# A decoder step on one core: sampled-attention copies, exponentials, convolution stores, turns and loads rearranged

## The chip, the core and the metric

The program runs on one NeuronCore of a Trainium2 chip. That core has five engines with an instruction stream each: TensorE (PE, the matrix products; its weight loads are shown apart as PEld), VectorE (DVE), ScalarE (ACT), GpSimd (POOL) and SyncE (SP), which here only issues transfers. An engine works through its stream in order and stops at an instruction whose operands aren't ready. Transfers between HBM and the on-chip memory SBUF run on DMA engines of their own; the products land in PSUM, of which the program keeps a few banks in rotation. The metric is the device time of one execution in microseconds, as the median of several runs.

## The reference

One inference step of a one-layer decoder, for 2048 new tokens of a prompt and for 8 sampled sequences with 8 new tokens each and 8192 cached ones. Everything is float32.

```python
z = x @ w_in                                   # one projection, 3600 columns
fq, fk, fv, flogf = ...                        # 8 attention heads of 64, with a forget gate
conv = conv_b + sum(xpad[:, j:j + S] * conv_w[j] for j in range(4))
mq, mk = split(silu(conv))                     # 4 mLSTM heads of 128
fox_h = softmax(q k^T / 8 + forget, causal) v  # prompt: 2048 keys; sampled: 8192 paged keys + 8 new ones
m_h   = mlstm(mq, mk, mv, ig, lf)              # chunked, with states C, n, m
mix = concat(fox_h, norm(m_h) * og) @ w_o
x1  = layer_norm(ALPHA * x + mix)
y   = layer_norm(ALPHA * x1 + square(relu(x1 @ w1)) @ w2)
```

Outputs are `y` for both token sets, the new keys, values and forget values, the mLSTM states and the convolution's last inputs.

## The kernel before

A float32 product is made of three products of rounded parts: every operand is split into a rounded high part (ACT, `split_hi`, line 149) and the rest (DVE, `split_lo`, line 152), and `mm3` (lines 157 to 159) multiplies high by high, low by high and high by low. So each piece of weights that comes in costs one ACT and one DVE pass before TensorE can use it.

The work has four stages, one after the other.

**Projection** (`block_a`, about 0 to 905 us), in four blocks of 512 tokens; the first block takes the 64 sampled tokens along. Each block does a first set of value columns, the columns that go through the convolution (`streamed`, in pairs of 128 columns with `ready` and `out`), then output gates, attention queries, keys and values. `pieces` goes over the weights in slabs of two or four 128-row chunks and for each slab over the token tiles; a `hook` may do something ahead of a tile's product. Before a block can begin, its tokens must be loaded (`x_load`), turned by TensorE (`x_turn`, line 370, into PSUM tile `px`) and split. The tiles `px` and `pm` share four PSUM banks; a bank comes free once ACT has copied the product in it (`stage`, line 587). The prompt's mLSTM (`m_block`) and the sampled one (`m_sample`) are generators of which a step is taken every 2.3 us of estimated product time (`PACE_M`, in `tick`); the sampled attention (`sample_attention`) is another generator, with a step every 5.6 us (`PACE_A`) here and every 5 (`PACE_C`) later.

**Prompt attention** (`phase_b`, about 905 to 1325 us): for a head and a group of 256 queries, `scores`, `weights` and `values`, a unit behind one another. `keys` doubles a head's keys (`dup`: a transfer, and a GpSimd copy for the second half, in `twice`), turns and splits them.

**Output projection** (`phase_o`, to about 1550 us) and the **MLP** (`phase_c`, `last_block`) follow. In the last tiles of the output projection the tokens of the first MLP block are turned (`x1_turn`, line 1403). The sampled attention goes on in these two stages.

`sample_attention` takes 32 steps a sequence. `k_gather` fetches 128 rows of keys by an indirect transfer from GpSimd, `k_turn` transposes them in place on DVE (line 2002), `qk_step` multiplies them (`sQ`, line 2025). At step 35 of a sequence `softmax` finds the maximum and takes ten exponentials one after the other (lines 2062 and 2064). `weights` (line 2094 on) then turns a quarter of them into PSUM tile `sT`, of which there is one, four transposes at a time, and copies the four into `PTs`: the copies of even number on DVE, the odd ones on ACT (line 2096). `pv_step` (`sO`, line 2137) multiplies `PTs` by values that were gathered by GpSimd (`v_gather`, line 2113).

The final order on each engine is made by a scheduler with a model of the time, from the data dependencies, the order in the code and `issue_after`, which holds an instruction behind another one. So a line's place in the code isn't its place in the stream.

Of the kernel before, what the change touches and what calls it, by code (L numbers as in the profile page):

```python
# [52 lines left out]
def body(ctx, tc, I, O, stages):  # L53
# [300 lines left out]
    def x_turn(bi, t):  # L354
# [12 lines left out]
        for hf in range(2):  # L367
            px = ppa.tile([128, 4, 128], F32, name="px", tag="pm", bufs=4)
            for k in range(4):
                T.transpose(px[:, k, :n], xn[:n, (hf * 4 + k) * 128:(hf * 4 + k + 1) * 128], ident[:n, :n])  # L370
# [145 lines left out]
    def block_a(bi):  # L516
# [26 lines left out]
        def pieces(sink, *cols, hook=None):  # L543
# [78 lines left out]
        J = {}  # L622

# [9 lines left out]
        def out(j, w, ps):  # L633
# [25 lines left out]
            if pre:  # L659
                ths = pa.tile([128, 64], F32, name="ths", bufs=1)  # L660
                conv(lambda q: J["qs"][:, :, q:q + 8], J["acs"], ths, ths)
                SY.dma_start(dqk[j], ths)
                V.tensor_copy(scT[:, j], J["qs"][:, :, 8:11])
# [4 lines left out]
        if pre:  # L668

# [82 lines left out]
    def b_first():  # L752
# [4 lines left out]
        G.tensor_copy(kn[:, :, 1], kn[:, :, 0])  # L757
# [6 lines left out]
        for g in range(4):  # L764
            for d in range(2):
                SY.dma_start(Bz["qn"][g][d * 64:d * 64 + 64], dq[0, 0:64, g * 256:(g + 1) * 256])
            if g == 1:
                SY.dma_start(kn[:, :, 0], O["k_prompt"].rearrange("l b s h d -> (l b s) (h d)")[512:1024, 0:64].rearrange("(i t) c -> t i c", t=128))
                G.tensor_copy(kn[:, :, 1], kn[:, :, 0])
# [64 lines left out]
    def m_block(bi):  # L834
# [7 lines left out]
        for _ in range(4):  # L842
# [229 lines left out]
    def phase_b():  # L1072
# [28 lines left out]
        def twice(src, t):  # L1101

            n = pb.tile([128, t, 2, 64], F32, name="dup", tag=f"dup{t}", bufs=3)
            SY.dma_start(n[:, :, 0], src.rearrange("(i t) c -> t i c", t=128))
            G.tensor_copy(n[:, :, 1], n[:, :, 0])
            return n

# [6 lines left out]

        def keys_load(h, g):
            return twice(kp[g * 512:(g + 1) * 512, h * 64:h * 64 + 64], 4)

        def keys(z, g):
# [3 lines left out]
            if not first:  # L1122
                kn = Bz["kn1"] if h == 0 and g == 1 else keys_load(h, g)
# [171 lines left out]
        for n in range(len(units) + 1):  # L1295
# [560 lines left out]
def sample_attention(tc, I, O, ps_, pps, cst, ident, sqk, dnl, dR, dmix, dqb, vx, kx, pe, ring_a):  # L1856
# [180 lines left out]
    def softmax(b):  # L2037
# [21 lines left out]
        for u in range(4):  # L2059
            for hg in range(2):  # L2060
                x = z["U"][u][:, hg].rearrange("p b k t -> p (b k t)")
                A.activation(x, x, AF.Exp, bias=m4[:, hg:hg + 1], accum_out=rp[:, hg, u:u + 1])
        for hg in range(2):
            A.activation(z["Sn"][:, hg], z["Sn"][:, hg], AF.Exp, bias=m4[:, hg:hg + 1], accum_out=rp[:, hg, 4:5])

    def softmax_new(b):

        z = state[b]
        rs = z["rs"] = ps_.tile([128, 2], F32, name="rs", bufs=2)
        V.tensor_reduce(rs, z["rp"], axis=AX.X, op=OP.add)  # L2070
# [15 lines left out]
    def weights(b, u, hg):  # L2086
# [8 lines left out]
        for f in range(4):  # L2095
            (A.copy if f % 2 else V.tensor_copy)(PT[:, hg, f].rearrange("p g h q -> p h g q"),
                                                 p[:, f].rearrange("p (h g q) -> p h g q", g=4, q=8))
# [72 lines left out]
    def step(n):  # L2170
# [30 lines left out]
        if b is not None and b < 8:  # L2201
            softmax_sum(b)
        u = at(n, 37, 8)
# [62 lines left out]
```

## Time and profile before

| | |
|---|---|
| median of three runs | 3270.63 us (3259.38 to 3270.8) |
| the profiled execution | 3264.98 us, of which the span from first to last instruction is 3263.1 |
| TensorE busy | 3174.9 us, 97% of the span |
| VectorE, ScalarE, GpSimd busy | 2230.5, 1393.6, 1049.9 us |
| mean granted TensorE clock | 0.990 |

The span is 88 us longer than TensorE is busy. The timeline of TensorE gives each of its waits with the engine that ended it; the table by windows shows the clock that was granted in a stretch, 1.00 being the full one.

### The profile page before, as it was taken

The page shows a single profiled execution, that of the slowest core. Times are in us where ns is not written, and L with a number is a line of the kernel's source. Part 1 is how long each engine was busy: PE and PEld are TensorE (multiplying, and loading weights), DVE is VectorE, ACT ScalarE, POOL GpSimd, SP SyncE. Part 2 cuts the span into 40 slices and gives each one's busy share as a digit, 9 for nine tenths or more (in the row PEclk, how much of TensorE's full clock was granted, in tenths as well). Part 3 has the DMA queues.
Part 4 walks back from the last instruction along what each step waited for, and adds up shares of the span by engine and source line. Part 5 has one row for each costly group of instructions (what it writes and reads, how often), then busy time and mean ns, then how long its engine had stood idle before and what let it go on. Part 6 is the DMA issues. An engine that isn't in the chain of part 4 may idle for free.

```text
span 3263.1 us, 54920 instructions
## 1 busy us (share of the span) xinstructions
PE 3174.9 (97%) x20140; PEld 2555.0 (78%) x20140; DVE 2230.5 (68%) x5239; ACT 1393.6 (43%) x2753; POOL 1049.9 (32%) x1171
## 2 busy tenths in 40 slices
PE   9999999999999999999999999999999999999998
PEld 8878787786777777777777777777777777799997
DVE  5857667666577777766566767666667545777777
ACT  4444244444377777412333333242423333454443
POOL 0011121432344444354333324323234210264441
PEclk9999999999999999999999999999999999999999
DMA  6565774977743224777686768776678645442221
GB/s 193 150 198 167 231 230 144 315 259 218 222 128 85 79 84 118 254 282 263 250 289 213 288 238 288 263 249 244 239 240 305 210 160 176 134 139 84 91 90 56
DMA packets 413845, 641.88 MB, mean 197 GB/s; under 512 B 83020, under 2 KB 295312, under 8 KB 412680
## 3 DMA queue, kind: packets, MB, share of 16 engines
q1 hardware_dynamic: 337320, 360.99, 36.4%
q0 software_dynamic: 74304, 270.57, 22.3%
q10 hardware_dynamic: 1952, 6.82, 0.6%
q8 instruction: 159, 2.61, 0.3%
q14 instruction: 110, 0.90, 0.1%
HBM read 585.43 MB, written 52.83 MB: 196 GB/s over the span
## 4 chain that ended last, share of the span: by engine, by line
PE 60%; DMA 5%; DVE 3%; issue 2%; POOL 1%; ACT 1%; SPq 0%; DVEq 0%; POOLq 0%; ACTq 0%
PE ph L157 7%; PE ph L158 7%; PE ph L159 7%; PE py L157 6%; PE py L159 6%; PE py L158 6%; PE po L1245 4%; PE pt L1228 4%; PE sO L2137 3%; PE pS L1187 2%; PE sQ L2025 2%; PE pS L1188 2%; DMA kT<-cache_k,idxK 2%; DMA xr<-cache_v,idxV 1%; PE pw L158 1%
## 5 line engine op out<-in xcount | busy, mean ns | idle before, releaser
L149 ACT ACTIVATE wh<-wr 128x1024 fp32r<-128x1024 f32 x268 | 277.6, 1056 | 538.2 <-PE py L159 299.8
L1996 POOL DMA_INDIRECT kT<-cache_k,idxK x256 | 262.3, 1025 | 741.1 <-PE sQ L2025 644.1
L2002 DVE STREAM_TRANSPOSE kT<-kT 128x512 f32<-128x512 f32 x512 | 330.2, 686 | 230.2 <-DMA kT<-cache_k,idxK 229.5
L157 PE MATMUL ph<-x1h,wh 128*128 128x512 f32 (+2 forms) x1280 | 453.5, 354 | 3.1 <-ACT xr L1664 2.1
L159 PE MATMUL ph<-x1h,wl 128*128 128x512 f32 (+2 forms) x1280 | 450.7, 354 | 6.0 <-DVE wl L152 6.0
L158 PE MATMUL ph<-x1l,wh 128*128 128x512 f32 (+2 forms) x1280 | 452.9, 354 | 0.0
L152 DVE TENSOR_TENSOR wl<-wr,wh 128x1024 fp32r<-128x1024 f32 x252 | 318.7, 1272 | 77.9 <-PE ph L159 45.8
L157 PE MATMUL py<-wh,h 128*128 128x512 f32 (+1 forms) x888 | 347.7, 395 | 0.8 <-DVE y L1807 0.3
L159 PE MATMUL py<-wh,h 128*128 128x512 f32 (+1 forms) x888 | 347.7, 392 | 0.0
L158 PE MATMUL py<-wl,h 128*128 128x512 f32 (+1 forms) x888 | 347.5, 392 | 0.0
L1607 DVE TENSOR_TENSOR y<-y,py 128x512 f32<-128x512 f32 x336 | 224.2, 677 | 142.6 <-PE py L159 140.6
L159 PEld LDWEIGHTS ph<-x1h,wl 128*128 128x128 f32 x1280 | 242.0, 189 | 38.9 <-DVE wl L152 7.1
L157 PEld LDWEIGHTS ph<-x1h,wh 128*128 128x128 f32 x1280 | 242.3, 189 | 38.1 <-ACT xr L1664 2.3
L158 PEld LDWEIGHTS ph<-x1l,wh 128*128 128x128 f32 x1280 | 242.1, 189 | 35.1 <-issue 2.5
L2113 POOL DMA_INDIRECT vt<-cache_v,idxV x156 | 160.6, 1030 | 291.0 <-PE sO L2137 252.1
L157 PE MATMUL pm<-whi,xhT 128*128 128x512 f32 (+2 forms) x648 | 235.7, 365 | 3.7 <-ACT acb L637 1.5
L158 PE MATMUL pm<-wlo,xhT 128*128 128x512 f32 (+2 forms) x648 | 230.7, 356 | 1.9 <-DVE wlo L152 1.9
L159 PE MATMUL pm<-whi,xlT 128*128 128x512 f32 (+2 forms) x648 | 230.6, 356 | 0.0
L157 PEld LDWEIGHTS py<-wh,h 128*128 128x128 f32 x888 | 167.1, 188 | 42.9 <-issue 7.8
L159 PEld LDWEIGHTS py<-wh,h 128*128 128x128 f32 x888 | 167.1, 188 | 36.2 <-issue 2.5
L158 PEld LDWEIGHTS py<-wl,h 128*128 128x128 f32 x888 | 167.1, 188 | 33.8 <-issue 2.9
L149 ACT ACTIVATE whi<-wra 128x1024 fp32r<-128x1024 f32 (+1 forms) x112 | 119.0, 1062 | 160.7 <-PE pm L159 105.6
(485 smaller groups left out, 7068.4 us busy)
## 6 DMA issues: line engine op xcount, KB each, us to landing
wr<-w SPq DMA_DIRECT2D x256, 512.0 KB
wra<-w_in SPq DMA_DIRECT2D x112, 512.0 KB
Rb<-dR SPq DMA_DIRECT2D x128, 128.0 KB
wr<-w_o SPq DMA_DIRECT2D x16, 512.0 KB
xr<-dmix SPq DMA_DIRECT2D x16, 512.0 KB
y<-x_prompt SPq DMA_DIRECT2D x16, 512.0 KB
dx<-y SPq DMA_DIRECT2D x16, 512.0 KB
qn<-dq SPq DMA_DIRECT2D x120, 64.0 KB
```

The costliest lines, as they stand in the source:

```text
L149: last["ACT"] = A.activation(dst, src, AF.Copy, scale=scale)
L152: r = (eng or V).tensor_tensor(dst, src, hi.bitcast(F32), op=OP.subtract)
L157: T.matmul(ps, wh, xh, start=first, stop=False, skip_group_check=free)
L158: T.matmul(ps, wh, xl, start=False, stop=False, skip_group_check=free)
L159: last["PE"] = T.matmul(ps, wl, xh, start=False, stop=stop, skip_group_check=free)
L1228: T.transpose(pt[:, k], sc[i][0][k0 // 8][:, (k0 % 8 + k) * 128:(k0 % 8 + k + 1) * 128], ident)
L1245: last["PE"] = T.matmul(po[c:c + 64, q0:], z["vn"][:, k], PTs[k // 4][:, k % 4, q0:], start=k == same[0], stop=k == same[-1], skip_group_c ...
L1607: V.tensor_tensor(y, y, ps, op=OP.add)
L1996: G.indirect_dma_start(out=piece(n), out_offset=None, in_=ck, in_offset=IO(ap=idxK[:, b, j // 2, j % 2:j % 2 + 1], axis=0))
L2002: V.transpose(x, x)
L2113: vx["last"] = G.indirect_dma_start(out=vt.rearrange("p f c -> p (f c)"), out_offset=None, in_=cv, in_offset=IO(ap=idxV[:, b, (kt % 4) * 4 ...
L2137: after_ = T.matmul(po[r:r + 32], z["PT"][:, hg, 2 * f + g, pg].rearrange("p h q -> p (h q)"), vts[f][:, g, hg * 256:(hg + 1) * 256], star ...
```

## The change

Line numbers here are those of the kernel before. Six edits, in the order of the code:

- **Turns.** `x_turn` returns its last transpose. For blocks 1 to 3 the first tile is turned ahead of the last tile's product of the last slab, and that product is held behind these transposes; the second tile is turned behind the last product.
- **Sampled convolution.** The eight results `ths` lie in one tile of eight slots and are stored by one transfer, not by eight from one reused tile.
- **First loads of prompt attention.** `b_first` is cut in two: the loads (`b_load`) are asked for at the first slab of the last value columns, the GpSimd copies and casts at the third slab's second tile.
- **`m_block`** waits six steps, not four, between asking for `gsb` and taking its exponential.
- **Keys.** The load (`keys_load`) and the GpSimd copy are parted; the load is asked for a unit earlier.
- **Sampled attention.** One ACT copy moves all four turned pieces into `PTs`. The exponentials are taken in four portions over steps 36 to 39, and the row sum is taken at step 40.

```diff
@@ x_turn
-                T.transpose(px[:, k, :n], xn[...], ident[:n, :n])
+                r = T.transpose(px[:, k, :n], xn[...], ident[:n, :n])
...
+        return r
@@ pieces
-                    if hook:
-                        hook(rows[0][0], i)
+                    r = hook(rows[0][0], i) if hook else None
                     if rows[0][0] == 0:
                         banks[t] = bank(t, n)
-                    part(banks[t], t, rows)
+                    with ExitStack() as es:
+                        if r is not None:
+                            es.enter_context(tc.issue_after(r.ins))
+                        part(banks[t], t, rows)
@@ convolution
+        if pre:
+            J["ths"] = ps_.tile([128, 8, 64], F32, name="ths", tag="vt", bufs=2)
...
-                ths = pa.tile([128, 64], F32, name="ths", bufs=1)
+                ths = J["ths"][:, j]
                 conv(lambda q: J["qs"][:, :, q:q + 8], J["acs"], ths, ths)
-                SY.dma_start(dqk[j], ths)
...
         if pre:
+            SY.dma_start(dqk.rearrange("j p t -> p j t"), J["ths"])
@@ turn_first
             if bi == 3:
-                if k == 4 and n == 0:
+                if k == 0 and n == 0:
+                    b_load()
+                if k == 4 and n == 1:
                     b_first()
                 return
...
-            if k == 6 and n == len(blk) - 2:
-                x_turn(bi + 1, BLKS[bi + 1][0])
+            if k == 6 and n == len(blk) - 1:
+                r = x_turn(bi + 1, BLKS[bi + 1][0])
                 x_load(BLKS[bi + 1][3])
-            if k == 6 and n == len(blk) - 1:
+                return r
+        pieces(halves(sink), (1024, 512), hook=turn_first)
+        if bi < 3:
+            with tc.issue_after(last["PE"].ins):
                 x_turn(bi + 1, BLKS[bi + 1][1])
-        pieces(halves(sink), (1024, 512), hook=turn_first)
@@ m_block
         va, Wm, qa = m_load(bi * 4)
-        for _ in range(4):
+        for _ in range(6):
             yield 1
         A.activation(gsb, gsb, AF.Exp)
@@ phase_b
+                if h == 0 and g in (1, 3):
+                    keys_load(0, g // 2 + 2)
+                if h < 7 and 3 <= g < 7:
+                    keys_load(h + 1, g - 3)
@@ weights of the sampled attention
-        for f in range(4):
-            (A.copy if f % 2 else V.tensor_copy)(PT[:, hg, f].rearrange("p g h q -> p h g q"),
-                                                 p[:, f].rearrange("p (h g q) -> p h g q", g=4, q=8))
+        A.copy(PT[:, hg].rearrange("p f g h q -> p f h g q"), p.rearrange("p f (h g q) -> p f h g q", g=4, q=8))
@@ step
+        b, u = divmod(n - 36, 32)
+        if 0 <= b < 8 and u < 4:
+            exps(b, u)
...
+        b = at(n, 40, 32)
+        if b is not None and b < 8:
+            z = state[b]
+            z["rs"] = ps_.tile([128, 2], F32, name="rs", bufs=2)
+            V.tensor_reduce(z["rs"], z["rp"], axis=AX.X, op=OP.add)
```

Three places in the streams that the scheduler made. The numbers behind the names tell the buffers apart.

TensorE, end of block 0 of the projection; `pm` with 512 columns is the last product of the value columns, `px` the turned tokens of block 1, `pm` with 256 columns block 1's first product. Before:

```order
L157 MATMUL pm_2561<-whi_2701,xhT_147 128x512
L158 MATMUL pm_2561<-wlo_2702,xhT_147 128x512
L159 MATMUL pm_2561<-whi_2701,xlT_148 128x512
L370 MATMUL px_2744<-ident_73,xn_2467 128x128 x4
L370 MATMUL px_2751<-ident_73,xn_2467 128x128 x4
L370 MATMUL px_2772<-ident_73,xn_2469 128x128 x4
L370 MATMUL px_2779<-ident_73,xn_2469 128x128 x4
L157 MATMUL pm_2810<-whi_2799,xhT_147 128x256
```

And of the change:

```order
L370 MATMUL px_2742<-ident_73,xn_2453 128x128 x4
L370 MATMUL px_2749<-ident_73,xn_2453 128x128 x4
L157 MATMUL pm_2547<-whi_2687,xhT_147 128x512
L158 MATMUL pm_2547<-wlo_2688,xhT_147 128x512
L159 MATMUL pm_2547<-whi_2687,xlT_148 128x512
...
L370 MATMUL px_2770<-ident_73,xn_2455 128x128 x4
L370 MATMUL px_2777<-ident_73,xn_2455 128x128 x4
L157 MATMUL pm_2796<-whi_2785,xhT_147 128x256
```

The six matmuls of the last tile's last slab now stand between the two turned tiles.

ScalarE, block 2 of the projection, around the exponential of `gsb` (`S` and `Sn` are the sampled exponentials, `qi`, `acb` and `hist` belong to the convolution, `whi` is a split of weights). Before:

```order
L2062 ACTIVATE S_5138,rp_5625<-S_5138,m4_5623 128x512 x2
L2064 ACTIVATE Sn_2860,rp_5625<-Sn_2860,m4_5623 128x8 x2
L653 ACTIVATE qi_5778<-acb_5394 128x512
L647 COPY hist_121<-qi_5800 128x3
L149 ACTIVATE whi_6055<-wra_6054 128x1024
L653 ACTIVATE qi_5800<-acb_5394 128x512
L844 ACTIVATE gsb_5973<-gsb_5973 128x16
L851 ACTIVATE Wm_5978<-Wm_5978,gm_98 128x128 x2
L2096 COPY PTs_5753<-sT_5754 128x4x4x8
```

And of the change:

```order
L2114 COPY PTs_5735<-sT_5742 128x4x4x4x8
L658 ACTIVATE qi_5776<-acb_5380 128x512
L631 COPY qi_5909<-hist_121 128x3
L648 COPY qi_5909<-pm_5843 128x512
L642 ACTIVATE acb_5380<-pm_5843,cw_112 128x512
L658 ACTIVATE qi_5862<-acb_5380 128x512
L652 COPY hist_121<-qi_5909 128x3
L658 ACTIVATE qi_5909<-acb_5380 128x512
L149 ACTIVATE whi_6088<-wra_6087 128x1024
L856 ACTIVATE gsb_5951<-gsb_5951 128x16
```

The exponential of `gsb` now stands behind the copy into `PTs` and behind the last convolution columns of the block, where before it stood ahead of both.

TensorE, the change from the output projection (`pw`) to the MLP (`ph`); `xr` and `y` are the rows that are turned for the first MLP block. Before:

```order
L159 MATMUL pw<-wh,ml 128x512
L2094 MATMUL sT<-ident,S 128x128 x4
L1403 MATMUL px<-ident,xr 128x128 x8
L1403 MATMUL px<-ident,y 128x128 x8
L2025 MATMUL sQ<-kT,qb 32x256 x16
L2137 MATMUL sO<-vt,PTs 32x256 x8
L157 MATMUL ph<-x1h,wh 128x512
```

And of the change:

```order
L159 MATMUL pw<-wh,ml 128x512
L1419 MATMUL px<-ident,xr 128x128 x8
L2041 MATMUL sQ<-kT,qb 32x256 x16
L2154 MATMUL sO<-vt,PTs 32x256 x8
L1419 MATMUL px<-ident,y 128x128 x8
L157 MATMUL ph<-x1h,wh 128x512
```

A step of the sampled attention has moved from behind the last turned row to ahead of it, and the four transposes `sT` to an earlier place.

More of the change, by code (lines that the diff above doesn't have):

```diff
@@ L1113, in forget_values @@
             SY.dma_start(z["vn"][:, a // 128:(a + n) // 128], vp[a:a + n, h * 64:h * 64 + 64].rearrange("(t p) c -> p t c", p=128))
+        KN = {}
         def keys_load(h, g):
-            return twice(kp[g * 512:(g + 1) * 512, h * 64:h * 64 + 64], 4)
+            n = KN[h, g] = pb.tile([128, 4, 2, 64], F32, name="dup", tag="dup4", bufs=3)
+            SY.dma_start(n[:, :, 0], kp[g * 512:(g + 1) * 512, h * 64:h * 64 + 64].rearrange("(i t) c -> t i c", t=128))
         def keys(z, g):
@@ L1122, in keys @@
             if not first:
-                kn = Bz["kn1"] if h == 0 and g == 1 else keys_load(h, g)
+                if h == 0 and g == 1:
+                    kn = Bz["kn1"]
+                else:
+                    kn = KN.pop((h, g))
+                    G.tensor_copy(kn[:, :, 1], kn[:, :, 0])
             if h == 0:
@@ L2058, in softmax, with exps @@
         rp = z["rp"] = ps_.tile([128, 2, 5], F32, name="rp", bufs=2)
-        for u in range(4):
+        z["m4"] = m4
+    def exps(b, u):
+        z = state[b]
+        for hg in range(2):
+            x = z["U"][u][:, hg].rearrange("p b k t -> p (b k t)")
+            A.activation(x, x, AF.Exp, bias=z["m4"][:, hg:hg + 1], accum_out=z["rp"][:, hg, u:u + 1])
+        if u == 0:
             for hg in range(2):
[L2061 to L2064, printed above, removed]
+                A.activation(z["Sn"][:, hg], z["Sn"][:, hg], AF.Exp, bias=z["m4"][:, hg:hg + 1], accum_out=z["rp"][:, hg, 4:5])
     def softmax_new(b):
         z = state[b]
-        rs = z["rs"] = ps_.tile([128, 2], F32, name="rs", bufs=2)
-        V.tensor_reduce(rs, z["rp"], axis=AX.X, op=OP.add)
         pn = z["pn"] = ps_.tile([8, 2, 32], F32, name="PTn", bufs=2)
```

15 lines of the change are left out of this document (6 added, 9 removed).

## Prediction

> **What bounds the kernel now.** I read the busy times first, then TensorE's timeline for its waits, then the windows behind the longest waits for the granted clock, and last what the engine that ended each wait had itself been waiting for.
>
> ```profile
> PE 3174.9 (97%) x20140; PEld 2555.0 (78%) x20140; DVE 2230.5 (68%) x5239; ACT 1393.6 (43%) x2753; POOL 1049.9 (32%) x1171
> ```
>
> TensorE is the bound; no edit takes a product away, so all there is to win is in the 88 us in which it is idle and in what its clock loses behind idle time. These are the waits at places that an edit touches (start, duration, instruction, and in brackets the idle time before it with the engine that ended it):
>
> ```profile
> 83.61 0.38 PE L157 MATMUL pm<-xhT,whi 128*128 128x256 f32 x1 [2.89 <-ACT acb L637]
> 236.41 0.66 PE L370 MATMUL px<-ident,xn 128*128 128x128 f32 x4 [2.37 <-ACT st L587]
> 238.28 0.58 PE L157 MATMUL pm<-whi,xhT 128*128 128x256 f32 x1 [1.21 <-DVE xlT L152]
> 443.71 0.66 PE L370 MATMUL px<-ident,xn 128*128 128x128 f32 x4 [0.95 <-ACT st L587]
> 447.81 0.66 PE L370 MATMUL px<-ident,xn 128*128 128x128 f32 x4 [1.25 <-ACT st L587]
> 551.32 0.62 PE L2137 MATMUL sO<-vt,PTs 128*32 128x256 f32 x2 [2.84 <-DVE PTs L2096]
> 553.45 0.80 PE L157 MATMUL pm<-whi,xhT 128*128 128x512 f32 x1 [1.51 <-ACT acb L637]
> 797.68 1.77 PE L2137 MATMUL sO<-vt,PTs 128*32 128x256 f32 x16 [4.19 <-DMA vt<-cache_v,idxV]
> 1547.11 0.66 PE L2094 MATMUL sT<-ident,S 128*128 128x128 f32 x4 [2.00 <-ACT PTs L2096]
> 1553.55 1.98 PE L1403 MATMUL px<-ident,y 128*128 128x128 f32 x8 [4.91 <-DVE x1l L152]
> 1557.22 3.64 PE L2025 MATMUL sQ<-kT,qb 128*32 128x256 f32 x32 [1.69 <-ACT PTs L2096]
> ```
>
> A long wait is paid for twice. The windows (length, then busy time and count of PE, PEld, DVE, ACT, POOL, then the granted clock, the DMA share and GB/s) show about half the clock behind them:
>
> ```profile
> 84.00:88.00 4.00, 4.00 (x21) 3.66 (x21) 3.89 (x13) 2.52 (x7) 0.00 (x0) 0.57 0.08 12
> 236.00:240.00 4.00, 2.38 (x12) 2.14 (x13) 4.00 (x8) 1.81 (x5) 0.91 (x5) 0.77 0.84 251
> 240.00:244.00 4.00, 4.00 (x30) 4.00 (x30) 0.07 (x2) 1.06 (x3) 0.00 (x0) 0.81 0.09 33
> 448.00:452.00 4.00, 3.74 (x32) 3.50 (x32) 3.84 (x12) 1.72 (x4) 0.00 (x0) 1.00 0.99 298
> 552.00:556.00 4.00, 2.55 (x6) 2.09 (x7) 2.54 (x4) 3.08 (x12) 1.92 (x2) 0.52 0.37 141
> 556.00:560.00 4.00, 4.00 (x12) 3.15 (x12) 3.38 (x6) 1.26 (x2) 0.00 (x0) 0.63 0.02 4
> 798.00:802.00 4.00, 4.00 (x25) 1.87 (x18) 2.59 (x6) 1.67 (x5) 1.07 (x5) 0.50 0.24 94
> 802.00:806.00 4.00, 4.00 (x13) 3.16 (x12) 4.00 (x11) 1.43 (x3) 2.61 (x3) 0.66 0.49 138
> 1552.00:1556.00 4.00, 1.98 (x8) 1.43 (x8) 4.00 (x6) 1.76 (x5) 2.35 (x1) 0.53 0.71 248
> 1556.00:1560.00 4.00, 2.78 (x28) 1.39 (x32) 3.03 (x6) 2.53 (x5) 0.56 (x1) 0.50 0.87 301
> ```
>
> Busy time times the missing clock gives the loss: 1.7 us behind the wait at 83.6 (4.00 x 0.43), 1.3 behind 236 to 238 (0.55 + 0.76), none behind the shorter ones at 444 to 448, 2.7 behind 551 to 553 (1.2 + 1.5), 3.4 behind 797.7 (2.0 + 1.4), 2.3 in the two windows of 1552 to 1560 (0.9 + 1.4).
>
> The Trainium skill ("TensorE: Matmul & The Clock Gate", section "What's actually happening") lets the clock fall to one half only after an idle window of about 3.4 us. The trace is stricter, since 2.89 us were enough at 83.6. By the page, the terms below would lose 1.7, 0.7 and 2.7 us of clock.
>
> **The change part by part.**
>
> *One store of the sampled convolution.* Eight stores go, one of eight times the size comes:
>
> ```profile
> 81.66 0.26 ACT L653 ACTIVATE ths<-acs 128x64 f32<-128x64 f32 x1 [7.11 <-DMA dqk<-ths]
> L662 SPq DMA_DIRECT2D dqk<-ths x8: 320/338/449, 59.0 to 118.1; - x8
> ```
>
> ACT could not write the single `ths` until the store before had read it, and stood 7.11 us; behind it stood the `acb` copies that free a bank, and TensorE waited 2.89. With a slot for each there is nothing to wait for. The new store is read only by the sampled mLSTM, much later, so it costs the path nothing. Gain 2.9 + 1.7 = **4.6 us**; bounds 2.9 (if another wait holds the clock down) and 4.6.
>
> *Turns.* Before, all sixteen transposes followed the last product, and the second tile's needed the bank that ACT had just begun to copy. Now six matmuls stand between the two tiles. They follow each other at this distance:
>
> ```profile
> 232.11 0.39 PE L158 MATMUL pm<-wlo,xhT 128*128 128x512 f32 x1
> 232.33 0.40 PE L159 MATMUL pm<-whi,xlT 128*128 128x512 f32 x1
> ```
>
> Six times 0.22 to 0.23 is 1.4 us in which ACT and DVE split the first tile. The second tile's bank still has to be copied after the product. At 236 to 238 the waits are 3.6 us, at 443 to 448 they are 2.2; I take half of each and half of the first one's clock loss: 1.8 + 1.1 + 0.65 = **3.6 us**. Bounds 0 (the copy of the last bank decides alone) and 7.1 (3.6 + 2.2 + 1.3). Behind the held product stands all of TensorE's stream; the two banks it now waits for were freed by products a tile or more earlier, so I cost the hold at nothing; if ACT is late there, the whole product waits with it.
>
> *`gsb` two steps later, and the copy into `PTs`.* At 551 the cause is again a blocked ACT:
>
> ```profile
> 550.00 0.22 ACT L844 ACTIVATE gsb<-gsb 128x16 f32<-128x16 f32 x1 [4.90 <-DMA gsb<-dgs]
> ```
>
> ACT stood 4.90 us for this small load, and behind it stood the copy for `sO` and the last `acb`. Two steps of 2.3 us are 4.6, and the order puts both ahead of `gsb`. So what is late then is only the prompt's mLSTM, which has a whole block's time. Gain 2.84 + 1.51 + 2.7 = **7.0 us**; bounds 1.5 (the value gather behind `sO` is late too) and 7.0.
>
> *One ACT copy for four.* It counts for the change from output projection to MLP:
>
> ```profile
> ACT PTs L2096 <- DVE PTs L2096: 215.3, 92, 11.0
> 1542.63 1.30 DVE L2002 STREAM_TRANSPOSE kT<-kT 128x512 f32<-128x512 f32 x2 [2.68 <-DMA kT<-cache_k,idxK]
> 1544.80 0.27 ACT L2096 COPY PTs<-sT 128x128 f32<-128x128 f32 x1 [4.98 <-DVE PTs L2096]
> L2096 DVE COPY PTs<-sT x128: 233/283/293, 540.3 to 2725.5; 128x128 f32<-128x128 f32 x128
> L2096 ACT COPY PTs<-sT x128: 238/266/285, 550.7 to 2725.8; 128x128 f32<-128x128 f32 x128
> 916.59 0.59 ACT L1231 COPY PT<-pt 128x512 f32<-128x512 f32 x1 [0.32 <-PE pt L1228]
> 1523.68 1.93 PE L2025 MATMUL sQ<-kT,qb 128*32 128x256 f32 x32
> 1557.07 1.09 ACT L149 ACTIVATE x1h<-px 128x512 fp32r<-128x512 f32 x2
> 1558.19 1.28 DVE L152 TENSOR_TENSOR x1l<-px,x1h 128x512 fp32r<-128x512 f32 x2
> ```
>
> DVE stood for gathered keys, its `PTs` copy behind that, ACT's behind DVE's, and `sT` behind ACT: over the span ACT waits 215 us for DVE so. With ACT alone, DVE loses 128 x 0.28 = 36 us of work, and ACT goes from 128 x 0.27 = 34 us to 64 copies at about 0.59 = 38; neither is the bound, so the work itself is worth nothing, the chain is. The waits of 2.00 and 1.69 go. Of the 4.91, the `sQ` now standing ahead covers 1.93 and the `sO` some 0.9; but `ph` then stands right behind the last turned rows and waits for their split, which `sQ` and `sO` covered before: ACT's first half (0.55) and DVE's two (1.28) are about 2. So 3.7 + 2.8 - 2.0 = 4.5, and half the clock loss, 1.2: **5.7 us**. Bounds 0 (DVE's wait for keys still decides) and 10.9 (8.6 + 2.3).
>
> *Loads of prompt attention.* At 797.7 the value gather was late because GpSimd stood for other loads:
>
> ```profile
> 787.53 0.40 POOL L773 CAST q<-acx 128x256 fp32r<-128x256 f32 x1 [1.56 <-DMA acx<-dq]
> ```
>
> The loads were already pulled far ahead of their place in the code, and in the new order one cast still stands between two value gathers, with the loads behind the same tile's last reader. I take **1 us**; bounds a loss of 2 (SP's three last loads now stand behind two loads of `Rb`) and a gain of 7.6 (4.19 + 3.4). The key loads that are now asked for earlier belong to prompt attention, where the timeline shows only short TensorE waits at its start, and the first of them hasn't moved on SP: nothing.
>
> *Exponentials in portions.* The same work in other places:
>
> ```profile
> L2062 ACT ACTIVATE S<-S,m x64: 706/709/731, 536.7 to 2568.6; 128x512 f32<-128x512 f32 x64
> ```
>
> Eight at 0.71 are 5.7 us of ACT in a row, under products before and after; the scheduler still puts most side by side. Nothing; at most a microsecond a sequence, 8 either way, which I put into the next term.
>
> *The rest.* Everything behind block 0 is laid out anew, up to the last block, and waits for gathers, of which these are some, fall elsewhere:
>
> ```profile
> PE sO L2137 <- DMA vt<-cache_v,idxV: 5.8, 3, 4.2
> ```
>
> One more such wait (1.9 on the mean of these three) with a clock loss of 3, as behind the long waits above, is a **loss of 5 us**; bounds 10 lost and none.
>
> Sum: 4.6 + 3.6 + 7.0 + 5.7 + 1 - 5 = 16.9, from the profiled 3264.98: **3248 us**. That execution lies 5.65 under the median of the runs shown and 5.6 over the lowest of them, in their middle, so I leave the number as it is.
>
> **Rivals.** *The waits only change places* (3260): the first term stays, but the other sites depend on how the new order meets gathers that it doesn't control. For it: most of the waits end on a transfer at the root. Against it: three edits each cut the very chain. 4.6 us are left, hence 3260.
>
> *All goes* (3228): every site to its upper bound, 4.6 + 7.1 + 7.0 + 10.9 + 7.6 = 37, nothing new.
>
> *ACT as the only server* (slower, 3298): in `weights`, one `sT` serves all; the second four transposes stand in TensorE's stream until ACT has copied the first four. ACT works in order and often stands for a product:
>
> ```profile
> ACT whi L149 <- PE pm L159: 105.6, 34, 6.9
> ```
>
> That is 3.1 us each. If 16 of the 32 pairs meet one, TensorE loses 50 us, less the 17: 3298. It decides from 6 pairs on (17 / 3.1). Against it: half the copies were on ACT before, and the list above has one wait of `sT` for them.
>
> *Half the clock only after some 3.4 us* (3253): the waits go but bring 5.1 us less (1.7 + 0.7 + 2.7). The windows behind the 2.89 us speak against it. The page of the Trainium skill named above ("TensorE: Matmul & The Clock Gate") states this rule.
>
> **How the numbers follow.** Forecast 0.53, waits changing places 0.22, all goes 0.12, ACT alone 0.10, the clock rule 0.03. About 0.5% (16 us) is what a measurement of this kernel can tell from no change: faster means under 3254.3, slower over 3287. The forecast's own spread, 3234 to 3258, puts 0.46 of its 0.53 under that line; with 0.12, 0.03 of the waits and 0.02 of the rule, faster is 0.63. ACT alone gives slower 0.07. The rest, 0.30, is the same. The range, 3230 to 3264, leaves out most of ACT alone and half of all goes.
>
> **What would show it.** Right: no ACT wait for `dqk`; no wait over 1 us before `pm` near 83 us; under 2 us at 236 and 1.5 at 444; none for `PTs` near 551; no ACT wait for another engine's `PTs` copy. Wrong: `sT` or `sO` waiting for ACT's copy of `PTs` in many places, `gsb` still holding ACT, the `px` transposes waiting ahead of the last product, or TensorE's idle time still near 88 us with new waits for gathers.

## Result and the profile after

The change makes the kernel 0.67% faster: 3245.68 us (median of six runs, 3236.88 to 3248.48) against 3267.73 (six runs, 3259.38 to 3270.8), a ratio of 0.9933, 95% interval 0.9919 to 0.9946. In a later set of runs the same pair gave 0.9943 (0.9924 to 0.9962). The forecast was 3248. The total came out nearly as the sum said, but in other places than the sum said, and that is what the experiments are about.

The busy times of the changed kernel (the page's first part): VectorE has lost the 36 us of copies, ScalarE has 4 us more, TensorE has the same instructions.

```profile
PE 3171.3 (98%) x20140; PEld 2553.6 (79%) x20140; DVE 2193.9 (68%) x5111; ACT 1397.6 (43%) x2689; POOL 1047.5 (32%) x1171
```

TensorE's waits in the changed kernel's timeline, at the places the prediction spoke of and at the new ones (start, duration, instruction, idle time before it and what ended it):

```profile
141.62 0.39 PE L157 MATMUL pm<-xhT,whi 128*128 128x256 f32 x1 [2.00 <-ACT st L715]
236.01 0.65 PE L370 MATMUL px<-ident,acx 128*128 128x128 f32 x4 [1.73 <-ACT st L590]
237.68 0.40 PE L157 MATMUL pm<-whi,xhT 128*128 128x256 f32 x1 [1.01 <-DVE xlT L152]
438.32 1.16 PE L874 MATMUL mm<-qk 128*128 128x128 f32 x8 [0.93 <-DVE Cs L907]
449.54 0.63 PE L370 MATMUL px<-ident,acx 128*128 128x128 f32 x4 [1.39 <-DVE xlT L152]
539.65 0.80 PE L157 MATMUL pm<-whi,xhT 128*128 128x512 f32 x1 [2.96 <-ACT acb L642]
758.56 1.94 PE L2154 MATMUL sO<-vt,PTs 128*32 128x256 f32 x16 [4.40 <-DMA vt<-cache_v,idxV]
795.59 1.94 PE L2154 MATMUL sO<-vt,PTs 128*32 128x256 f32 x16 [3.42 <-DMA vt<-cache_v,idxV]
1545.15 1.93 PE L1419 MATMUL px<-ident,y 128*128 128x128 f32 x8 [3.27 <-DVE x1l L152]
1548.45 0.79 PE L158 MATMUL ph<-x1l,wh 128*128 128x512 f32 x1 [0.75 <-DVE x1l L152]
2415.75 1.94 PE L2154 MATMUL sO<-vt,PTs 128*32 128x256 f32 x16 [5.05 <-DMA vt<-cache_v,idxV]
```

The wait at 83 us is gone, and so are those for `PTs` near 551, 1547 and 1557. But there are 2.96 us at 539.7 for the convolution's `acb`, 4.40 at 758.6 for gathered values, and 5.05 at 2415.8 for them again. The wait at 141.62 is one that the kernel before has too, later:

```profile
146.57 0.39 PE L157 MATMUL pm<-xhT,whi 128*128 128x256 f32 x1 [1.83 <-ACT st L710]
```

Three stretches of each kernel tell where the time went: up to the long wait for `acb`, from there to the first product of prompt attention, and from the first wait of the output projection to the sampled rows at the MLP's end. First the windows of the kernel before (length, then busy time and count of PE, PEld, DVE, ACT, POOL, clock, DMA share, GB/s):

```profile
0.00:553.45 553.45, 529.46 (x3286) 448.67 (x3286) 375.08 (x1038) 237.58 (x549) 86.62 (x113) 0.99 0.64 189
553.45:905.02 351.57, 342.81 (x2274) 267.75 (x2274) 220.34 (x596) 143.73 (x348) 116.95 (x130) 0.98 0.77 246
1340.87:2781.94 1441.07, 1411.30 (x8812) 1088.33 (x8812) 932.22 (x1791) 474.25 (x764) 477.08 (x460) 0.99 0.71 247
```

And of the changed kernel:

```profile
0.00:539.65 539.65, 521.96 (x3259) 443.99 (x3260) 368.85 (x1030) 231.29 (x533) 84.66 (x112) 0.99 0.64 190
539.65:903.78 364.13, 350.16 (x2299) 272.05 (x2300) 219.50 (x580) 149.42 (x351) 120.20 (x128) 0.97 0.75 243
1338.55:2764.40 1425.85, 1407.82 (x8813) 1086.75 (x8813) 902.17 (x1687) 478.60 (x712) 473.30 (x460) 1.00 0.71 250
```

Idle time of TensorE is length less busy time. Up to `acb` it fell from 24.0 to 17.7 us; from there to prompt attention it rose from 8.8 to 14.0. So in these two profiles the projection won 6.3 us and gave 5.2 back, and prompt attention begins at 903.8 instead of 905.0. From 1340 us on, with the same work (8812 and 8813 matmuls), idle time fell from 29.8 to 18.0 and busy time by 3.5, which is clock: 15.2 us, nearly all of the profiled gain of 17.6.

### The profile page after: what moved, and what is told of

Read it like the earlier page. It is cut to its first block, busy times and chain, and to the rows that moved or that the text cites. A ratio compares the mean times of both kernels' runs of the same rounds, so it can differ in the third digit from the quotient of the medians.

```text
span 3245.5 us, 54623 instructions
## 1 busy us (share of the span) xinstructions
PE 3171.3 (98%) x20140; PEld 2553.6 (79%) x20140; DVE 2193.9 (68%) x5111; ACT 1397.6 (43%) x2689; POOL 1047.5 (32%) x1171
## 4 chain that ended last, share of the span: by engine, by line
PE 64%; issue 12%; DMA 11%; DVE 7%; POOL 4%; ACT 2%; SPq 0%; DVEq 0%; POOLq 0%; ACTq 0%
DMA kT<-cache_k,idxK 6%; PE ph L159 5%; PE ph L157 5%; PE ph L158 5%; PE py L157 5%; PE py L158 5%; PE py L159 5%; PE po L1257 4%; PE pt L1240 4%; PE pm L157 3%; PE pm L159 3%; PE pm L158 3%; PE sO L2154 2%; PE pS L1199 2%; PE sQ L2041 2%
## 5 line engine op out<-in xcount | busy, mean ns | idle before, releaser
L152 DVE TENSOR_TENSOR wlo<-wra,whi 128x1024 fp32r<-128x1024 f32 (+1 forms) x112 | 136.5, 1221 | 63.9 <-ACT whi L149 63.4
```

The source lines that it names most:

```text
L152: r = (eng or V).tensor_tensor(dst, src, hi.bitcast(F32), op=OP.subtract)
```

## Experiments: which part carries it

The question was what carries those 15 us, and why the projection's parts bring so little. Theory A: the one ACT copy carries the late gain. B: the portioned exponentials do. C: neither, and any new layout of the streams moves the time by as much. Each part was set apart.

**Only the one ACT copy.**

```diff
 (kernel before)
-        for f in range(4):
-            (A.copy if f % 2 else V.tensor_copy)(...)
+        A.copy(PT[:, hg]..., p...)
```

> Only the one ACT copy into PTs is made; everything else stays as before (3267.7 us). The whole change saved 22 us at the median, and by the marks of the two traces some 15 of the 17.6 us of span were saved behind 1340 us, in the output projection and the MLP. Theory A (the copy carries that gain: ACT no longer waits for VectorE's half of the copies, 215 us over the span): about 3252, a ratio of 0.995, with the saving between 1340 and 2780 us. Theory B (the portioned exponentials carry it): 3267, ratio 1.000. Theory C (no single part carries it; any new layout of the streams moves the waits for gathers by some 5 to 15 us): anywhere from 3255 to 3275, and the saving at no particular place. In all three ACT's row of waits for VectorE's PTs copy (215.3 us) is gone.

**Only the portions.** The kernel before with `exps` called for a quarter at each of the steps 36 to 39 and the row sum at step 40.

> Only the exponentials are taken in portions over four steps, with the row sum later; the copies into PTs stay shared by VectorE and ACT. Theory A: no change, 3265 to 3270, ratio 0.999 to 1.001, since they are the same 64 instructions of 0.71 us. Theory B: about 3252, ratio 0.995. Theory C: anywhere from 3255 to 3275.

**Only the projection's parts.** The kernel before with one store, turns, `gsb` two steps later, `b_load` and `keys_load`.

> Only the projection's parts are made (one store, turns, gsb two steps later, earlier loads of prompt attention and of keys); sampled attention is as before. My prediction gave these parts 4.6 + 3.6 + 7.0 + 1.0 us, less 5 for new waits: 3256, ratio 0.9965. But in the trace of the whole change the first product of prompt attention came only 1.2 us earlier. Theory A (they win their waits, and give them back at new waits for value gathers near 758 and 796 us, whatever stands behind): 3264 to 3268, ratio 0.999 to 1.000, first product of prompt attention 1 to 3 us earlier. Theory D (the waits near 758 us belong to the sampled attention's part of the change alone): first product some 10 us earlier, 3256, ratio 0.9965.

**All but the copy.** The changed kernel with the four shared copies put back.

> The whole change without the one ACT copy: the four pieces are copied by VectorE and ACT in turn, as before. Theory A: most of the gain is gone, 3262 to 3268, ratio about 0.999 to the kernel before, and ACT waits some 200 us for VectorE's PTs copies again. Theory B: the gain stays, about 3247, ratio 0.9935. Theory C: anywhere from 3245 to 3270.

Measured against the kernel before (3268.15 us in this set): the copy alone 3261.92, ratio 0.9980 (0.9966 to 0.9993); the portions alone 3265.68, 0.9988 (0.9976 to 1.0001); the projection's parts alone 3263.10, 0.9978 (0.9961 to 0.9994); all but the copy 3256.14, 0.9955 (0.9938 to 0.9972). The copy is worth 6 us alone. On top of the rest it is worth 8 to 10 by the medians (3256.14 against 3248.03 and 3245.68), but the intervals of these ratios overlap. So neither A (15) nor B in its pure form holds for the times, and C's wide ranges hold all three kernels for which it was stated. The three parts alone add up to 14 us, the whole change to 22. The stages say more. Up to prompt attention and from the output projection to the MLP's end, in the windows of the copy alone and then of the projection's parts alone:

```profile
0.00:909.60 909.60, 872.08 (x5558) 717.79 (x5558) 590.18 (x1609) 381.57 (x883) 206.00 (x241) 0.98 0.68 210
1344.36:2772.09 1427.73, 1410.87 (x8813) 1089.37 (x8813) 905.45 (x1687) 477.60 (x712) 476.12 (x460) 0.99 0.71 249
```

```profile
0.00:900.96 900.96, 870.39 (x5559) 716.01 (x5559) 595.84 (x1633) 379.89 (x895) 198.03 (x240) 0.99 0.69 212
1335.49:2779.81 1444.32, 1413.96 (x8812) 1089.51 (x8812) 930.09 (x1791) 474.71 (x764) 474.15 (x460) 0.99 0.70 247
```

The copy alone has nearly the whole late gain (1427.7 against 1441.1 us) and is 4.6 us later at the mark of 905. (The profiled execution is its fastest of twelve, 7.6 us under its median.) The projection's parts alone have none of the late gain and are 4.1 us earlier at 905. That is theory A for the place. The differences at 905 are less certain. Up to 538 us the copy alone has the streams of the kernel before, instruction for instruction, and it is 2.9 us behind there already, so in these two profiles only 1.7 of the 4.6 us arose where the streams differ.

TensorE's list of waits in the late stretch (us in total, times, longest) shows what the copy changed there. First the kernel before, then the copy alone:

```profile
PE px L1403 <- DMA xr<-dx: 6.4, 2, 5.6
PE ph L159 <- DVE wl L152: 3.0, 2, 2.5
PE sT L2094 <- ACT PTs L2096: 2.0, 1, 2.0
PE sQ L2025 <- ACT PTs L2096: 1.7, 1, 1.7
```

```profile
PE sT L2094 <- ACT PTs L2095: 1.7, 1, 1.7
PE px L1403 <- DMA xr<-dx: 1.2, 2, 0.8
PE ph L159 <- DVE wl L152: 0.3, 1, 0.3
```

The wait for the rows `xr` is short with all but the copy too (1.2 us) and long with both variants below (6.3), so it isn't the copy's. The wait for `wl`, the split of weights on VectorE, is: in the ten profiles of the table further down it comes to 2.7 to 3.5 us in the six without the one copy and to 0.3 to 1.0 in the four with it. No single wait carries the gain.

In the projection the copy alone has a new wait, and an old one kept:

```profile
769.31 1.93 PE L2135 MATMUL sO<-vt,PTs 128*32 128x256 f32 x16 [4.80 <-DMA vt<-cache_v,idxV]
806.12 1.07 PE L2135 MATMUL sO<-vt,PTs 128*32 128x256 f32 x16 [2.21 <-DMA vt<-cache_v,idxV]
```

With the projection's parts alone no value gather ends a long wait there (the wait at 794.60 is 4.26 us for ACT's exponentials instead). I read this so: the `sO` products behind the copies are now ready sooner, and the values are not. ScalarE's last copy ahead of the wait of 4.40 begins at 730.3 us, the matching one of the kernel before at 747.7. In the changed kernel the gather that ends the wait of 4.40 was asked for at 742.88 and 744.12 (timeline of GpSimd); by the view of the tile `vt`, the median of the three gathers asked for in 735 to 760 us took 13.7 us to land:

```profile
742.88 0.94 POOL L2130 DMA_INDIRECT vt<-cache_v,idxV  x1 [1.07 <-PE sO L2154]
744.12 0.93 POOL L2130 DMA_INDIRECT vt<-cache_v,idxV  x1 [0.30 <-issue]
```

```profile
DMA to landing us min/median/max: 5.2/13.7/14.4
```

The gather is asked for once the `sO` before it has freed a place, so it can't run further ahead of the products when these become ready sooner. The Trainium skill ("DMA: Bandwidth & Descriptors", "Anatomy of one DMA — SWDGE (gpsimd) path") fits a transfer by 2.0 us and its bytes at 436 GB/s, which for 128 rows of 1024 values (0.52 MB) would be an estimate of 3.2 us. The measured 5 to 14 us are far more. The DMA engines' share is 0.91 in 748 to 754 us, but the kernel before has 0.91 as well (760 to 766 us), and its value gathers in 735 to 805 us took 4.0 to 7.9 us. Why these took longer isn't shown.

The copy alone also waits 1.71 us for values at 576.5 and 2.08 at 687.9 for a bank (ACT's `st`), two places where the kernel before has no wait over 0.9 us. For the projection's parts alone, the time (3263.10) lies nearer theory A's range there (3264 to 3268) than D's 3256, but the waits that took the gain back aren't the value gathers that A named: they are 3.52 us for `acb` at 544.2 and the 4.26 for exponentials.

## Experiments: place, engine and bunch

The next four runs were on another chip. On it the kernel before takes 3347.39 us, and its stretch from the output projection to the MLP's end is 73 us longer. The ratios are to runs on that chip. The whole change itself was not run there, so a variant can be set against it only across chips.

**The kernel before, profiled again.**

> The kernel before, unchanged, profiled once more: how far do the places of the stages move between two executions of one program? The stage marks of the first profile are 905.0 us (first product of prompt attention), 1340.9 (first wait of the output projection), 1553.6 (last turned rows of it) and 2781.9 (sampled rows of the MLP). If they hold within 1.5 us, the marks of the other kernels can be read to that; if they move by 4 or more, a stage's gain of a few us in one profile proves nothing.

Prompt attention began at 906.45, the output projection's first wait ended at 1344.78. So the first mark holds within 1.5 us here, and the second is 3.9 off.

**The copy only from the output projection on.**

```diff
 (changed kernel)
-        A.copy(PT[:, hg]..., p...)
+        if kx.get("late"):
+            A.copy(PT[:, hg]..., p...)
+        else:
+            for f in range(4):
+                (A.copy if f % 2 else V.tensor_copy)(...)
```

`late` is set as the output projection begins.

> The whole change, but in the projection the copies into PTs stay shared by VectorE and ACT; the one ACT copy begins with the output projection. In the profiles the one copy alone saved 13.4 us behind 1341 us and lost 4.6 us before 905 us, where new waits for gathered values stand (4.80 us at 769, 2.21 at 806). If the place decides (the copy is good where VectorE is crowded, bad where ACT holds the convolution's copies and the gathers are late), the first product of prompt attention comes at 900 to 902 us and the rest is as with the whole change: 3240 to 3244, ratio 0.992 to 0.993. If the whole change's projection is no worse for the copy, 3245 to 3248, ratio 0.9935.

3330.93 us, ratio 0.9944 (0.9923 to 0.9966), not better than the whole change on its chips. Prompt attention began at 891.6, earlier than expected, with no value wait over 1 us ahead of it. The place of the copies doesn't explain that: up to this mark the kernel has the streams of *all but the copy*, instruction for instruction, and there prompt attention began at 902.2. One order thus gave two profiles that lie 10.6 us apart at this mark (`sT` waits 1.25 us for exponentials near 785 here, 4.24 near 795 there, and TensorE is 8.6 us less busy with the same products). A few us at this mark, read from one profile, prove nothing. From the output projection on nothing was won: 1512.5 us against 1513.9 of the kernel before on this chip.

**One copy on VectorE instead of ACT.**

```diff
 (kernel before)
-        for f in range(4):
-            (A.copy if f % 2 else V.tensor_copy)(...)
+        V.tensor_copy(PT[:, hg]..., p...)
```

> The kernel before with one VectorE copy of all four pieces in place of the four shared ones: the chain between the two engines is gone as with the one ACT copy, but the work stays on VectorE. If the chain from VectorE over ACT to TensorE was the loss (my prediction), about the same gain as with the one ACT copy: 3262, ratio 0.998, and the MLP about 10 us shorter. If what counts is that VectorE loses work in the MLP (its 36 us of copies) or that TensorE's sT no longer waits on VectorE, no gain or a loss: 3266 to 3275, ratio 1.000 to 1.002.

3341.45 us, ratio 0.9977 (0.9955 to 0.9999): as with the ACT copy in the total. The late stretch, however, was 1518.2 us, no shorter than before, and since the ACT copy wins nothing there on this chip either, the run does not tell the chain from the unloading of VectorE. What it does show is that the new wait is not ACT's doing: again `sO` waited for values, 2.16 us at 767.9 and 4.27 at 801.8. Prompt attention began at 910.4. All five profiles in which one engine makes the copies in the projection have a wait for values between 752 and 770 us; none of the nine profiles that share the copies there, on three chips, has one.

**Portions eight steps apart.** In the changed kernel the four portions stand side by side in ACT's stream all the same (timeline of ACT: first and last exponential, and the copy behind them for which TensorE waits):

```profile
532.02 0.73 ACT L2082 ACTIVATE S<-S,m 128x512 f32<-128x512 f32 x1
...
537.55 0.71 ACT L2082 ACTIVATE S<-S,m 128x512 f32<-128x512 f32 x1
...
538.82 0.78 ACT L642 ACTIVATE acb<-pm,cw 128x512 f32<-128x512 f32 x1
```

```diff
 (changed kernel)
-        b, u = divmod(n - 36, 32)
-        if 0 <= b < 8 and u < 4:
-            exps(b, u)
+        u = at(n, 36, 8)
+        if u is not None and u < 32:
+            exps(u // 4, u % 4)
 (row sum at step 64, its product at 65)
```

> The whole change, with the four portions of exponentials eight steps apart instead of one (each just ahead of the turn that reads it; the row sum at step 64). In the changed kernel all ten exponentials still stand side by side on ACT (532.0 to 538.3 us), and behind them the acb copy for which TensorE waits 2.96 us at 539.7. If the bunch is what replaced gsb as the blocker, that wait goes (under 1 us at 540), with some 1.5 us of clock: 3 to 5 us less before 905 us, 3240 to 3243, ratio 0.992. If ACT is late there for another reason, the wait stays and the time is that of the whole change, 3246, ratio 0.9935.

3325.44 us, ratio 0.9928 (0.9903 to 0.9953). The bunch is open (ACT's timeline of this run):

```profile
532.63 0.72 ACT L2082 ACTIVATE S<-S,m 128x512 f32<-128x512 f32 x1
553.94 0.71 ACT L2082 ACTIVATE S<-S,m 128x512 f32<-128x512 f32 x1
```

Between 450 and 560 us, where the changed kernel has its 2.96, no TensorE wait over 0.2 us is left. The next one is 2.46 us at 563.0, for ACT's `st`, where the changed kernel has none. Prompt attention began at 899.3. So the bunch of exponentials was what held `acb` at 540. It had stood in front of that copy in the kernel with only the projection's parts too (3.52 us at 544.2): taking `gsb` out of the way had let the next blocker through. In the total the gain doesn't show: 0.9928 against 0.9933, on different chips.

## Experiments: what a new layout is worth

These runs were on a third chip, on which the kernel before takes 3267.72 us, as on the first.

**Both variants together.** Portions eight steps apart and the copy only from the output projection on.

> The whole change with both variants: copies into PTs shared as before until the output projection begins and one ACT copy after it, and the portions of exponentials eight steps apart. Apart, the first brought the first product of prompt attention to 891.6 us and the second to 899.3, against 903.8 with the change as it is. If the two gains are of different waits (value gathers near 758 and 796 us; the bunch of exponentials near 540 us) they add: first product at 886 to 891 us, and the time some 12 to 17 us, 0.4 to 0.5%, under that of the whole change: ratio to the kernel before 0.988 to 0.9895. If both only lay the streams out anew, the ratio stays at 0.993.

3242.83 us, ratio 0.9925 (0.9906 to 0.9944): not under 0.9895. Prompt attention began at 900.2, not at 886 to 891. The wait at 540 is gone here too and no value wait stands near 758, but `sT` waits 4.65 us at 791.3 for ACT's exponentials. In the total the gains didn't add. For the stage the profiles can't say. Up to 537 us this kernel has the same streams as the run above with only the portions eight steps apart; there it is 6.5 us behind that run's profile, and at prompt attention 0.9.

**The whole change again.**

> The whole change as it is, on the same chip as the others of this set: ratio 0.993 to the kernel before, as measured (0.9919 to 0.9946). Its marks: first product of prompt attention within 3 us of 903.8, with value gathers ending TensorE waits of 3 to 5 us near 758 and 796 us again if these belong to the order and not to one execution.

3248.03 us, 0.9943 (0.9924 to 0.9962). Prompt attention began at 905.8, with waits for values of 3.83 and 2.96 us at 761 and 798: they belong to the order, not to one execution. The late stretch took 1427.3 us. *Both* lies 5 us under this, which the two intervals don't separate.

**The kernel before with one number changed.**

```diff
-PACE_M = 2.3
+PACE_M = 2.35
```

> The kernel before with one number changed by 2%: a step of the prompt's mLSTM every 2.35 us instead of 2.3. No work, wait or buffer is added or taken away, but the streams of the projection are laid out anew. If a new layout alone moves the time by 0.3% or more either way, the gains of single parts (0.1 to 0.2%) can't be told from it: ratio anywhere from 0.996 to 1.004. If the layout is worth less than that, 0.999 to 1.001.

3288.44 us, ratio 1.0069 (1.0045 to 1.0093): 21 us slower, as much as the whole change wins, and more than the 0.4% that was allowed for. Nearly all of it lies in the projection, where prompt attention began 18.5 us later; the late stretch is 2 to 3 us longer:

```profile
0.00:923.54 923.54, 879.56 (x5559) 722.13 (x5559) 595.44 (x1633) 380.63 (x895) 201.14 (x241) 0.98 0.68 207
1360.87:2804.85 1443.98, 1410.70 (x8812) 1089.32 (x8812) 929.72 (x1791) 473.67 (x764) 476.95 (x460) 0.99 0.71 247
```

Idle time up to 905 us was 32.7 in the kernel before and is 44.0 here, and 7 us more of busy time, for the same products, are lost clock. It is one new layout, and a slower one; whether others come out faster wasn't tried, nor is it on record whether 2.3 had been chosen for this order. TensorE's timeline shows waits that came with nothing but a shift of the prompt's mLSTM steps by 2%:

```profile
145.83 0.55 PE L157 MATMUL pm<-xhT,whi 128*128 128x256 f32 x1 [4.15 <-DVE st L690]
457.08 0.58 PE L157 MATMUL pm<-whi,xhT 128*128 128x256 f32 x1 [4.84 <-ACT st L587]
831.14 0.77 PE L884 MATMUL mn<-va,Wm 128*128 128x129 f32 x2 [4.52 <-issue]
```

**The kernel before, a third profile.**

> The kernel before once more, for marks on the same chip as the three others: first product of prompt attention at 905 to 907 us as in the two earlier profiles (905.0 and 906.5).

Prompt attention began at 903.7, and the late stretch took 1442.1 us.

Put together for the first and the third chip, from the same windows of each profile (the copy is the one ACT copy behind 1340 us; for the first profiles of *before* and *whole change* the chip isn't on record):

```
kernel                 portions  copy   to prompt att.  late stretch  idle in it
before                    -       -        905.0          1441.1        29.8
before, again             -       -        903.7          1442.1        29.8
projection's parts        -       -        901.0          1444.3        30.4
pace 2.35                 -       -        923.5          1444.0        33.3
portions alone           yes      -        912.4          1432.1        26.5
all but the copy         yes      -        902.2          1437.7        28.5
copy alone                -      yes       909.6          1427.7        16.9
whole change             yes     yes       903.8          1425.9        18.0
whole change, again      yes     yes       905.8          1427.3        20.5
both variants            yes     yes       900.2          1427.8        19.6
```

The late stretch falls into three groups by the sampled attention's form, with 2 to 6 us within a group. The portions without the copy bring 7 to 9 us there (against the projection's parts, and against the kernel before). The copy alone brings 13 to 14, on top of the rest 10 to 12, and both together no more than the copy. The first column follows nothing of the kind: it runs from 900 to 924, the pace alone moves it by more than any edit, and one order gave 902.2 and, on the second chip, 891.6.

## Why the prediction was right in the sum and wrong in its terms

- *One store (4.6).* Right where it stands. No wait is left near 83 us, and no ACT wait for `dqk` in any of the seven profiles with it. The next wait ended at 146.57 before and ends at 141.62 now, 4.95 us sooner. In the seven profiles without the one store it ends at 145.8 to 147.8, in the seven with it at 140.5 to 143.0.
- *Turns (3.6).* Too much. At 236 to 238 there were 3.58 us and are 2.74, at 443 to 452 there were 2.71 and are 2.32 (of which 0.93 for another tile): 1.2 us without the clock. The bank still has to be copied after the product, which was the lower bound given.
- *`gsb` (7.0).* The wait for it went, as said, and with it `sO`'s wait for `PTs`. The step that failed is "what is late then is only the prompt's mLSTM": ten exponentials stood next in ACT's stream, and TensorE waited 2.96 us at 539.7, where it had waited 2.84 and 1.51. The gain was about 1.4 us of wait.
- *Exponentials in portions (0).* The reason given, that the scheduler puts them side by side, was right for the projection: they stayed the block that took the place of `gsb`. The *nothing* was wrong for the late stretch, where portions without the copy bring 7 to 9 us. Why, the runs don't show. Beside the copy, as in the whole change, they bring 0 to 2 us more there (1425.9 and 1427.3 against 1427.7), so in this sum it did no harm.
- *One ACT copy (5.7).* The place that I priced came out close: at the change to the MLP 2.00 + 4.91 + 1.69 = 8.6 us of waits became 3.27 + 0.75 = 4.0, where I had worked out 4.5 less. But I priced a chain of 215 us at one place only. Over the late stretch the copy took 8 to 13 us of idle time, and the stretch is 10 to 14 us shorter with it. This is the term that was mis-sized, by some 5 to 9 us. That the copy alone is worth 6 us in the total, about the 5.7 of the sum, does not bear the sum out: its profile shows 13 us won in the late stretch and 4.6 lost before 905. Between the chain and VectorE's lost 36 us of work the cause is open: the VectorE copy, which was to tell them apart, ran where neither form wins in that stretch.
- *Loads of prompt attention (1).* Not shown. The value wait at 797.7 went from 4.19 to 3.42, nearly as forecast, but other executions of the two kernels have 3.47 and 3.02 before and 2.96 with the change.
- *The rest (-5).* The kind was right, one more wait for gathered values in the projection (4.40 us). It is not luck of the layout, however: it comes with the copies being made by one engine. What a new layout can do is far larger than the bounds of 10 and none: the pace changed by 2% cost 21 us.

The terms that I put into the projection sum to 16.2, less the 5 to 11.2. The first pair of profiles shows 1.2 there, the second pair a loss of 2.1 (905.8 against 903.7). The output projection and the MLP gave 15.2 and 14.8 where I had 5.7. The two errors cancelled, which is luck. That the sum lay within 3 us of the median is therefore no proof of its terms.

*ACT as the only server* is refuted: six pairs of waits were its point, and in the changed kernel `sT` never waits for ACT's copy. With the copy alone it does so twice, 3.64 us at 551.3 and 1.68 at 1489.9. ACT stands for TensorE's transposes instead (ACT's list of waits; before, the row was 215.3 us for VectorE):

```profile
ACT PTs L2114 <- PE sT L2113: 101.5, 26, 9.6
```

*Half the clock only after some 3.4 us*, the rule of the Trainium skill ("TensorE: Matmul & The Clock Gate", "What's actually happening"), is refuted as a bound: behind the 2.96 us at 539.7 the clock is half, and even behind 2.00 at 141.6 it is 0.72:

```profile
141.00:144.00 3.00, 2.38 (x14) 2.38 (x15) 2.47 (x13) 1.90 (x6) 0.00 (x0) 0.72 0.39 137
540.00:543.00 3.00, 3.00 (x8) 2.35 (x8) 3.00 (x5) 2.96 (x8) 0.00 (x0) 0.50 0.31 99
```

*All goes* failed where waits stayed: 2.74 us at 236 to 238, 2.96 at 539.7 and 4.0 at the change to the MLP.

*The waits only change places* is what happened in the projection. It was wrong for the whole only because the copy won behind it.

## What to carry to other kernels

Price a chain between engines over every place where it stands, not at the one wait that shows it best. When a blocker is taken from an in-order queue, look at what stands beside it in the queue, since that can be the next wait. Where a scheduler lays the streams out anew, change a number that adds and removes no work and time that first: here it moved the time by as much as six edits together. Read a gain of that size stage by stage, from several profiles, and compare the order of the streams before you credit a part: where two kernels still have the same order, what lies between their profiles is not the edit's.

## What was not expected of the hardware

On the second chip the same program took 3347 us instead of 3268. All but 5 us of the 77 in the profiled spans lie between the output projection and the MLP's end (1513.9 us against 1441.1), where idle time was 71.3 us instead of 29.8 and busy time 31 us more. Many of the new waits ended on nothing that the profile shows:

```profile
PE sQ L2044 <- issue: 13.3, 16, 1.8
```

What bounds it there the runs don't show. On that chip the profiles of the two variants of the change show nothing won in that stretch, and are ahead by the projection, which ended 7 to 15 us earlier; on the other chips it was the other way round. The profiled executions there lie 5 us under (the kernel before), 7 under and 5 over (the variants) the medians of their kernels, so it is only a hint that much the same ratio can come from different stages.
